# A Macaron block with RWKV-7 mixer: SP loads in a planned order, the first 128 rows first in the head, and the last 128 rows' output shared by three engines

## The chip, the cores and the metric

The kernel runs on one core of one Trainium2 chip. The time is that of one execution on the device, in microseconds; a lower time is better. The median of 3 runs of the kernel before is 2033.16 us (2027.96, 2033.72 and 2033.16).

The page of the profile names five engines: PE (TensorE, the matrix engine; its weight loads are listed apart as PEld), DVE (VectorE), ACT (ScalarE), POOL (GpSimd) and SP (SyncE, which only issues transfers). Sixteen DMA engines move the data for all of them.

## The reference

There are 256 tokens of width 2048, all in float32. Three sublayers are added to the residual stream `h` in turn:

```python
f = _swiglu(_rmsnorm(h, ffn1_pre), gate1, up1, down1);  h = h + 0.5 * _rmsnorm(f, ffn1_post)
m = _hybrid_mixer(_rmsnorm(h, mix_pre), ...);           h = h + _rmsnorm(m, mix_post)
f = _swiglu(_rmsnorm(h, ffn2_pre), gate2, up2, down2);  h = h + 0.5 * _rmsnorm(f, ffn2_post)

def _swiglu(x, wg, wu, wd): return (silu(x @ wg) * (x @ wu)) @ wd        # D_FF = 5632

def _hybrid_mixer(u, ...):
    z_a, z_b, g_a, g_b = split(u @ w_in)           # 3360, 1024, 2048 and 2048 columns
    y_a = _rwkv7_branch(z_a, ...) @ w_proj_a       # 16 heads of 64, a recurrence over the tokens
    y_b = _pool_branch(z_b, ...) @ w_proj_b        # means over windows of 2, 4, 8 and 16 tokens
    return (sigmoid(g_a) * y_a + sigmoid(g_b) * y_b) @ w_out
```

## The kernel before

**Products in three parts.** Every float32 operand is split into two parts of a shorter float format, high and low. A weight tile `w` comes from DRAM; ScalarE casts it to `wH`; VectorE subtracts to get `wL`. The activations have `xH` and `xL` in the same way. A product is then three matmuls (`mm3`: high by high, low by high, high by low). The input of each product is 128 rows of the contraction by 128, and the other operand is 512 wide. The 256 tokens are two halves `h` of 128 rows. The tile names in the rows tell the stage: `f` and `l` are the gate and the up product and, in the down product, two column groups; `mm` is a product with the token rows on the output's partitions; `tr` is a transpose on TensorE; `pS`, `pA`, `pk`, `Z`, `mz` belong to the mixer's recurrence, the "chain".

**The planner.** Nothing is issued as the program text stands. Each engine call (`Engine.__getattr__`, line 78, which is why nearly every row of the profile carries line L477, where the plan is written out) is recorded by `Plan.add` with a cost (`Plan.cost`), a nominal time `nom` (the sum of the paces of the main stream of matmuls so far) and a slack `lag`. `Plan.deadlines` gives it a due time `dl` from those who use its result. `Plan.simulate` then walks through time with a model of the five engines and the buffers, and on each engine but TensorE takes the operation with the earliest due time that is ready in the model; `Plan.emit` writes the five orders out. On TensorE the main stream keeps the program's order, and two other streams ("side" for transposes, "chain" for the recurrence) are slipped in. In the real execution each engine works strictly through its written order, so an instruction that waits holds all behind it. In the model a transfer takes its bytes at 387 per ns and lands `LAND` = 1600 ns later. `s.set(lag=..., behind=...)` changes slack, or adds a dependence, for what is recorded inside it.

**Buffers.** `w` has 5 buffers, `wH` and `wL` 5 each; all larger temporaries share 34 "units".

**Stages.** `Kernel.ffn` runs the gate and up products in 11 blocks of 512 columns, then `down`. The first gate block of the first FFN is preceded by `head` (line 675): it loads `x` in four column pieces `c` for each of the two row halves (`load(h, c)`), transposes them (`turn(h, c)`), fetches (`get`) and splits (`split(k)`) the weight tiles, and calls `do(k, h)`, the three matmuls of contraction tile `k` for row half `h`. Sixteen transposes of an identity (`WARM`) run first, and eight more (`WARM2`) behind `turn(1, 0)`. The activation of a block returns to the transposed layout by a round trip to DRAM: the tile `T` is stored to `cx` and loaded back as `x` (`carry`), then cast to `xH`/`hH` on ScalarE.

`Kernel.mixer` runs the parts of `MIX_ORDER` and, in `ev_pa`, multiplies the gate tile `sga` by `y_a @ w_proj_a` and adds `mb`, the gated second branch, which had been stored to DRAM (`msp`). The first two of the four column blocks return by `carry`, the last two by transposes (`tr<-ident,sga`). Then comes `w_out`.

**Loads from GpSimd.** `post` (line 1082) ends each sublayer: it loads the norm's weights `gb` as a broadcast row, calls `reload()` (the residual rows `xr`, `h1`, `h2`, four transfers of 512 KB by `load_to`), and after the last column group finishes the four 128x512 output pieces of each half: `fg * r + resid` on VectorE, followed by `emit`, which in the last sublayer stores to `out`. The loads of `gb`, `mb` and the reloads are issued from GpSimd's queue. All weights, `cx` and the stores to `out` go from SP; in the head the pieces `c = 0` of `x` go from ScalarE. `setup_mixer` (the mixer's constant columns, `cols`, and their transposes `pr`) is run from `s.after` behind the first up product.

Of the kernel before, what the change touches and what calls it, by code (L numbers as in the profile page):

```python
# [82 lines left out]
SYNC = 55.0  # L83
LAND = 1600.0
SWITCH = 170.0
RUN = 16
# [7 lines left out]
class Plan:  # L94
# [109 lines left out]
    def cost(s, o, name, w, r, k):  # L204
# [33 lines left out]
        elif o.eng == "DVE":  # L238
            f = 1 / 0.96
            if name in ("tensor_copy", "tensor_scalar") and not psum:  # L240
                f /= 2
            more = 45.0 if name == "scalar_tensor_tensor" else 26.0 if name == "transpose" \
                else 40.0 if name == "tensor_tensor_scan" or n < 256 else 0.0
            o.pace, o.dur = n * f + 75 + more, n * f + 158 + more
        else:
            o.pace = o.dur = {"tensor_tensor": 400 + 160.0 * n,
                              "tensor_copy": 450.0}.get(name, n + 110.0)
# [35 lines left out]
    def simulate(s):  # L283
# [20 lines left out]
        gate = {e: [] for e in engines}  # L304
        prog, cfg, held = 0.0, (0, 0), None

# [35 lines left out]
        def go(o):  # L342
# [20 lines left out]
            if o.nbytes:  # L363
                dma = max(now + 1900, dma) + o.dur
                o.end = dma + LAND
            else:
                o.end = now + dur
# [21 lines left out]
        while done < len(ops):  # L389
            moved = True  # L390
            while moved:
                moved = False
                for e in engines:
                    if free[e] > now:
                        continue
                    w, av = wait[e], avail[e]
# [94 lines left out]
class Block:  # L491
    def __init__(s, tc, ctx):
# [3 lines left out]
        s.n = 0  # L496
        s.after = []
        s.cp = E(tc.tile_pool(name="cp", bufs=1))
# [176 lines left out]
    def head(s, w, c0, KT, do, keep, xs):  # L675
# [10 lines left out]
        for _ in range(WARM):  # L686
            s.nc.tensor.transpose(ps[:, :P], s.ident, s.ident)
        load(None, None)
        load(0, 0)
        load(1, 0)  # L690
        for k in range(4):
            get(k, 1)
        for c in range(1, 4):
            load(0, c)
            get(4 * c, 2)
            load(1, c)
            get(4 * c + 2, 2)
        split(0)
        turn(0, 0)
        split(1)  # L700
        last = turn(1, 0)
        split(2)
        split(3)
        with s.set(behind=last):
            for _ in range(WARM2):
                s.nc.tensor.transpose(ps[:, :P], s.ident, s.ident)
        for k in range(KT):
            do(k, 0)
            last = do(k, 1)
            if k % 2 == 0 and k + 4 < KT:  # L710
                turn(k // 2 % 2, k // 4 + 1)
                split(k + 4)
            if k == SQ:
                late = last
        with s.set(behind=late):
# [209 lines left out]
class Kernel(Block):  # L925
# [28 lines left out]
    def ffn(s, wg, wu, wd, uT, rs, gpost, resid, emit, reload, xs=None):  # L954
# [33 lines left out]
        s.gemm_tok(wu, 0, at, NKD, hold(1))  # L988
        while s.after:
            s.after.pop(0)()  # L990
        rb = s.rtmp("rsb")
# [8 lines left out]
        for b in range(1, nb):  # L1000
            J = jobs[b]
            s.block_seq(J, jobs.get(b + 1), evac([1.0, 1.0] if b > 1 else rs, [], J.banks))
        s.down(wd, s.T_at(hT), NKF, s.post(gpost, 0.5, resid, emit, reload), hT, sm,
# [11 lines left out]
    def normed(s, uT, rb, su):  # L1015
# [66 lines left out]
    def post(s, gpost, fac, resid, emit, reload):  # L1082
# [18 lines left out]
        def ev(c, h, ps):  # L1101
            if h == 0 and c % 2 == 0:
                nc.gpsimd.dma_start(out=gb[c // 2], in_=gpost[c * 512:c * 512 + 1024]
                                    .partition_broadcast(P))
# [4 lines left out]
            if c == 3:  # L1109
                r = s.small(1, "rs", bufs=8)  # L1110
                with s.set(lag=100.0):
# [3 lines left out]
                    for q in range(4):  # L1115
                        o = cc_(fg[h], q)
                        nc.vector.scalar_tensor_tensor(out=o, in0=o, scalar=r,
                                                       in1=resid(h, q), op0=ALU.mult,
                                                       op1=ALU.add)
                        emit(h, q, o)  # L1120
                return
# [181 lines left out]
    def mixer(s, prm, uT, rs, resid, emit, gpost, reload):  # L1303
# [517 lines left out]
def kernel(tc, x, ln_ffn1_pre, ln_ffn1_post, ffn1_gate, ffn1_up, ffn1_down,  # L1821
# [11 lines left out]
    with ExitStack() as ctx:  # L1833
# [11 lines left out]
        def load(h, c):  # L1845
            if h is None:
                with s.set(lag=-20000.0):
                    nc.sync.dma_start(out=gr, in_=ln_ffn1_pre[0].rearrange("(k p) -> k p", p=P))
# [37 lines left out]

        def emit(h, c, ap):
            nc.sync.dma_start(out=out[0, h * P:h * P + P, c * 512:c * 512 + 512], in_=ap)
        s.ffn(ffn2_gate[0], ffn2_up[0], ffn2_down[0], uT3, rs3, ln_ffn2_post[0],
# [35 lines left out]
```

## Time and profile before

| | value |
|---|---|
| median of 3 runs | 2033.16 us |
| the profiled execution's own time | 2032.8 us |
| its span in the trace | 2031.1 us |
| mean granted TensorE clock | 0.995 |
| matmuls and transposes on PE | 9837 |
| moved by DMA | 470.91 MB |

The rows of the profile are quoted in the prediction. A row of the waits reads: the engine and the tile it worked on next, what ended its wait, the total in us, how often, the longest. A row of a timeline reads: start and duration in us, engine, line, operation, out<-in, count, and in brackets the idle time of the engine just before, with what ended it. A stretch (a row of the windows) gives the busy time of each engine with the number of its instructions, then the clock granted to TensorE, the busy share of the DMA engines and what they moved.

### The profile page before, as it was taken

Reading aid. Unit: us, or ns where it says so; the run is one execution under the profiler, and the core shown is the slowest. Engines: PE = TensorE matmul, PEld = TensorE weight load, DVE = VectorE, ACT = ScalarE, POOL = GpSimd, SP = SyncE. Lnnn points to the kernel's source line nnn. Section 1 sums busy time; section 2 is a strip of 40 time slices with the busy share of each in tenths; the row PEclk is TensorE's granted clock in tenths of the full one; section 3 lists DMA queues with packets and bytes.
Section 4 is the critical chain, followed back from the end, with each engine's and each line's share of the span. In section 5 each row is a group of like instructions: output and inputs, shape, how many; then the busy total and the mean of one; then the engine's idle time right before and its main releaser. Section 6 shows DMA issues by size and latency. Waiting matters only on the chain.

```text
span 2031.1 us, 28147 instructions
## 1 busy us (share of the span) xinstructions
PE 2002.6 (99%) x9837; PEld 1655.5 (82%) x9837; DVE 1744.9 (86%) x2278; ACT 1185.6 (58%) x1588; POOL 80.9 (4%) x148
## 2 busy tenths in 40 slices
PE   9999999999999999999999998999999999999998
PEld 7888888888888888887887786888888888788886
DVE  7989999999888758897868768898899999998885
ACT  7555656565555556864845444575556565655552
POOL 0000000000001110001200110010000000000000
PEclk9999999999999999999999998999999999999999
DMA  7688888887667686656575576657888888876674
GB/s 270 228 260 266 283 267 273 273 278 227 206 205 255 220 245 212 196 178 189 153 229 179 168 232 198 229 199 237 260 263 284 264 275 270 270 228 214 198 258 138
DMA packets 254855, 470.91 MB, mean 232 GB/s; under 512 B 20592, under 2 KB 43258, under 8 KB 254714
## 3 DMA queue, kind: packets, MB, share of 16 engines
q1 hardware_dynamic: 248537, 448.68, 68.5%
q0 software_dynamic: 5888, 19.93, 2.9%
q8 instruction: 77, 1.26, 0.3%
q10 hardware_dynamic: 288, 0.52, 0.1%
q14 instruction: 65, 0.52, 0.1%
HBM read 444.40 MB, written 24.64 MB: 231 GB/s over the span
## 4 chain that ended last, share of the span: by engine, by line
PE 68%; DVE 13%; DMA 8%; issue 5%; ACT 4%; SPq 1%; DVEq 0%; POOL 0%; ACTq 0%; POOLq 0%
PE l L477 23%; PE f L477 20%; PE mm L477 18%; DVE wL L477 6%; PE p L477 5%; DMA x<-cx 3%; DMA w<-in_ffn_gate_dram 3%; ACT wH L477 2%; DVE t L477 2%; SPq L477 1%; DMA w<-in_ffn_up_dram 1%; DVE w L477 1%; DMA w<-in_w_proj_a_dram 1%; DVE T L477 1%; PE tr L477 0%
## 5 line engine op out<-in xcount | busy, mean ns | idle before, releaser
L477 ACT CAST wH<-w 128x1024 fp32r<-128x1024 f32 (+2 forms) x722 | 748.2, 1047 | 625.9 <-PE mm L477 142.8
L477 DVE TENSOR_TENSOR wL<-w,wH 128x1024 fp32r<-128x1024 f32 (+2 forms) x722 | 864.6, 1211 | 162.3 <-ACT wH L477 158.5
L477 PE MATMUL l<-wL,xH 128*128 128x512 f32 x788 | 307.1, 390 | 0.0
L477 PE MATMUL l<-wH,xH 128*128 128x512 f32 x788 | 306.9, 389 | 0.0
L477 PE MATMUL l<-wH,xL 128*128 128x512 f32 x788 | 306.6, 389 | 0.0
L477 PE MATMUL f<-wL,xH 128*128 128x512 f32 x672 | 261.7, 389 | 0.2 <-DVE wL L477 0.2
L477 PE MATMUL f<-wH,xL 128*128 128x512 f32 x672 | 261.6, 389 | 0.0
L477 PE MATMUL f<-wH,xH 128*128 128x512 f32 x672 | 261.4, 389 | 0.0
L477 PE MATMUL mm<-wH,xH 128*128 128x512 f32 (+1 forms) x672 | 261.0, 388 | 0.0
L477 PE MATMUL mm<-wH,xL 128*128 128x512 f32 (+1 forms) x672 | 260.9, 388 | 0.0
L477 PE MATMUL mm<-wL,xH 128*128 128x512 f32 (+1 forms) x672 | 260.6, 388 | 0.1
L477 PEld LDWEIGHTS l<-wL,xH 128*128 128x128 f32 x788 | 147.9, 188 | 31.5 <-DVE wL L477 0.7
L477 PEld LDWEIGHTS l<-wH,xH 128*128 128x128 f32 x788 | 147.9, 188 | 30.6
L477 PEld LDWEIGHTS l<-wH,xL 128*128 128x128 f32 x788 | 147.9, 188 | 30.2
L477 DVE TENSOR_TENSOR t<-w,w 128x1024 f32<-128x1024 f32 (+1 forms) x156 | 158.5, 1016 | 16.1 <-DMA w<-in_ffn_down_dram 8.3
L477 PEld LDWEIGHTS f<-wL,xH 128*128 128x128 f32 x672 | 126.1, 188 | 27.0 <-DVE wL L477 0.7
L477 PEld LDWEIGHTS f<-wH,xH 128*128 128x128 f32 x672 | 126.2, 188 | 26.1
L477 PEld LDWEIGHTS f<-wH,xL 128*128 128x128 f32 x672 | 126.2, 188 | 26.1
L477 PEld LDWEIGHTS mm<-wH,xL 128*128 128x128 f32 x672 | 126.2, 188 | 25.0
L477 PEld LDWEIGHTS mm<-wL,xH 128*128 128x128 f32 x672 | 126.2, 188 | 25.0 <-DVE wL L477 0.5
L477 PEld LDWEIGHTS mm<-wH,xH 128*128 128x128 f32 x672 | 126.2, 188 | 24.5
L477 DVE TENSOR_TENSOR wL<-t,wH 128x1024 fp32r<-128x1024 f32 x96 | 116.8, 1217 | 5.5 <-ACT wH L477 5.1
(308 smaller groups left out, 2679.4 us busy)
## 6 DMA issues: line engine op xcount, KB each, us to landing
w<-in_w_in_dram SPq DMA_DIRECT2D x128, 512.0 KB
w<-in_ffn_up_dram SPq DMA_DIRECT2D x116, 512.0 KB
w<-in_ffn_gate_dram SPq DMA_DIRECT2D x114, 512.0 KB
w<-in_ffn_down_dram SPq DMA_DIRECT2D x112, 512.0 KB
w<-in_ffn_gate_dram SPq DMA_DIRECT2D x184, 256.0 KB
w<-in_ffn_up_dram SPq DMA_DIRECT2D x180, 256.0 KB
w<-in_ffn_down_dram SPq DMA_DIRECT2D x128, 256.0 KB
cx<-T SPq DMA_DIRECT2D x31, 512.0 KB
```

What stands on the lines that cost most here:

```text
L477: ins = o.fn(*[real(x) for x in o.a], **{n: real(x) for n, x in o.k.items()})
```

## The change

1. **The planner's model.** SP may not issue while the transfer eight back has not landed in the model (`LANES`). A transfer that depends on a transfer lands `CARRY` = 1800 ns later. GpSimd's `tensor_tensor` with 64 or more columns costs 300 + n ns instead of 400 + 160n.
2. **The queue of loads.** `gb`, `mb` and the reloads go from SP instead of GpSimd, at the place that the planner gives them. Stores to `hsp` and `msp` stay on GpSimd.
3. **The head.** All its loads carry an explicit order. The first piece of `x` comes in two halves, one from ScalarE and one from SP, and all others from SP. The products of the first 128 rows with contraction tiles 0 and 1, and the eight `WARM2` transposes, come before or around the transposes of the second 128 rows. `setup_mixer` runs at block 3, and the first additions in `normed` wait for a matmul of the head.
4. **The tail.** For the last 128 rows of the last sublayer, the first output piece is done and stored in two halves of 256 columns, and the third is multiplied on ScalarE and added on GpSimd. Each has a lag that sets its order.

The planner lays out everything anew, so that other orders change as well, the interleaving of the chain with the mixer's products among them; the main stream of TensorE changes its order only in the head.

```diff
+LANES = 8
+CARRY = 1800.0
...
-            o.pace = o.dur = {"tensor_tensor": 400 + 160.0 * n,
+            o.pace = o.dur = {"tensor_tensor": 400 + 160.0 * n if n < 64 else 300.0 + n,
...
                 o.end = dma + LAND
+                if any(ops[q].nbytes for q in o.preds):
+                    o.end += CARRY
+                if e != "POOL":
+                    lanes.append(o.end)
+                    heapq.heappush(events, (o.end, next(rel), None))
...
+                    if e == "SP" and len(lanes) >= LANES and lanes[-LANES] > now:
+                        continue
...
+        seq = itertools.count()
+
+        def first(fn, *a):
+            with s.set(lag=-30000.0 + 300 * next(seq)):
+                fn(*a)
+        first(load, None, None)
+        first(load, 0, 0)
+        first(get, 0, 1)
+        first(get, 1, 1)
+        first(load, 1, 0)
+        first(get, 2, 1)
+        first(get, 3, 1)
...
         split(0)
-        turn(0, 0)
-        split(1)
-        last = turn(1, 0)
-        split(2)
-        split(3)
+        last = turn(0, 0)
         with s.set(behind=last):
             for _ in range(WARM2):
                 s.nc.tensor.transpose(ps[:, :P], s.ident, s.ident)
+        do(0, 0)
+        split(1)
+        do(1, 0)
+        turn(1, 0)
+        do(0, 1)
+        split(2)
+        do(1, 1)
+        split(3)
...
-        while s.after:
-            s.after.pop(0)()
...
+            while s.after and b == 3:
+                s.after.pop(0)()
...
-            V.tensor_tensor(out=fl(x), in0=fl(uH).bitcast(F32), in1=fl(uL).bitcast(F32),
-                            op=ALU.add)
+            with s.set(behind=s.late):
+                V.tensor_tensor(out=fl(x), in0=fl(uH).bitcast(F32), in1=fl(uL).bitcast(F32),
+                                op=ALU.add)
...
-                nc.gpsimd.dma_start(out=gb[c // 2], in_=gpost[c * 512:c * 512 + 1024]
+                nc.sync.dma_start(out=gb[c // 2], in_=gpost[c * 512:c * 512 + 1024]
...
+                        m = 1 if q else 2
+                        for i in range(m):
+                            b = slice(i * 512 // m, (i + 1) * 512 // m)
+                            with s.set(lag=600.0 * (q + q + i) - 6000.0):
+                                if q == 2:
+                                    nc.scalar.mul(o, o, r)
+                                    nc.gpsimd.tensor_tensor(out=o, in0=o, in1=x, op=ALU.add)
+                                else:
+                                    nc.vector.scalar_tensor_tensor(
+                                        out=o[:, b], in0=o[:, b], scalar=r, in1=x[:, b],
+                                        op0=ALU.mult, op1=ALU.add)
+                                emit(h, q, o[:, b], b)
...
-                    nc.gpsimd.dma_start(out=mbs[c], in_=msp[c])
+                    nc.sync.dma_start(out=mbs[c], in_=msp[c])
...
-            (nc.sync if c else nc.scalar).dma_start(
-                out=at_tok(xs)(h, c), in_=x[0, h * P:h * P + P, c * 512:c * 512 + 512])
+            o = at_tok(xs)(h, c)
+            for q, e in ((0, nc.scalar), (1, nc.sync)) if h + c == 0 else ((None, nc.sync),):
+                b = slice(0, 512) if q is None else slice(q * 256, q * 256 + 256)
+                e.dma_start(out=o[:, b], in_=x[0, h * P:h * P + P, c * 512:c * 512 + 512][:, b])
...
-                        nc.gpsimd.dma_start(out=dst[h][c],
-                                            in_=src(h)[:, c * 1024:c * 1024 + 1024])
+                        nc.sync.dma_start(out=dst[h][c],
+                                          in_=src(h)[:, c * 1024:c * 1024 + 1024])
```

More of the change, by code (lines that the diff above doesn't have):

```diff
@@ L304, in simulate @@
         gate = {e: [] for e in engines}
-        prog, cfg, held = 0.0, (0, 0), None
+        prog, cfg, held, lanes = 0.0, (0, 0), None, []
         def can(o):
@@ L496, in __init__ @@
         s.n = 0
-        s.after = []
+        s.after, s.final = [], False
         s.cp = E(tc.tile_pool(name="cp", bufs=1))
@@ L687, in head @@
             s.nc.tensor.transpose(ps[:, :P], s.ident, s.ident)
[L688 to L692, printed above, removed]
+        seq = itertools.count()
[9 more added lines that the diff above has]
+        first(get, 3, 1)
         for c in range(1, 4):
[L694 to L697, printed above, removed]
+            first(load, 0, c)
+            first(get, 4 * c, 2)
+            first(load, 1, c)
+            first(get, 4 * c + 2, 2)
         split(0)
-        turn(0, 0)
-        split(1)
-        last = turn(1, 0)
-        split(2)
-        split(3)
+        last = turn(0, 0)
         with s.set(behind=last):
@@ L706, in head @@
                 s.nc.tensor.transpose(ps[:, :P], s.ident, s.ident)
+        do(0, 0)
[6 more added lines that the diff above has]
+        split(3)
         for k in range(KT):
-            do(k, 0)
-            last = do(k, 1)
+            if k > 1:
+                do(k, 0)
+                last = do(k, 1)
             if k % 2 == 0 and k + 4 < KT:
@@ L713, in head @@
             if k == SQ:
-                late = last
+                s.late = late = last
         with s.set(behind=late):
@@ L1115, in ev @@
                     for q in range(4):
[L1116 to L1120, printed above, removed]
+                        o, x = cc_(fg[h], q), resid(h, q)
+                        if not (s.final and h):
+                            nc.vector.scalar_tensor_tensor(out=o, in0=o, scalar=r, in1=x,
+                                                           op0=ALU.mult, op1=ALU.add)
+                            emit(h, q, o)
+                            continue
+                        m = 1 if q else 2
[8 more added lines that the diff above has]
+                                        out=o[:, b], in0=o[:, b], scalar=r, in1=x[:, b],
+                                        op0=ALU.mult, op1=ALU.add)
+                                emit(h, q, o[:, b], b)
                 return
@@ L1846, in load @@
             if h is None:
-                with s.set(lag=-20000.0):
-                    nc.sync.dma_start(out=gr, in_=ln_ffn1_pre[0].rearrange("(k p) -> k p", p=P))
+                nc.sync.dma_start(out=gr, in_=ln_ffn1_pre[0].rearrange("(k p) -> k p", p=P))
                 ps = s.psum("pg1")
@@ L1885, with emit @@
                 load_to(h1, lambda h: hsp[0, h]))
-        def emit(h, c, ap):
-            nc.sync.dma_start(out=out[0, h * P:h * P + P, c * 512:c * 512 + 512], in_=ap)
+        def emit(h, c, ap, b=slice(0, 512)):
+            nc.sync.dma_start(out=out[0, h * P:h * P + P, c * 512:c * 512 + 512][:, b], in_=ap)
+        s.final = True
         s.ffn(ffn2_gate[0], ffn2_up[0], ffn2_down[0], uT3, rs3, ln_ffn2_post[0],
```

## The prediction

> **What bounds the kernel now.** I read the page first, then the waits of TensorE, the stretches around the longest of them, and the timelines there. All times are microseconds.
>
> ```profile
> span 2031.1 us, 28147 instructions
> PE 2002.6 (99%) x9837; PEld 1655.5 (82%) x9837; DVE 1744.9 (86%) x2278; ACT 1185.6 (58%) x1588; POOL 80.9 (4%) x148
> ...
> PE tr L477 <- DVE sga L477: 8.5, 1, 8.5
> PE pS L477 <- ACT Z L477: 2.9, 1, 2.9
> PE tr L477 <- DMA x<-in_x_dram: 1.7, 1, 1.7
> PE l L477 <- DVE hL L477: 1.4, 2, 1.2
> PE pr L477 <- DMA cols<-in_pool_scale_dram: 0.5, 1, 0.5
> ```
>
> TensorE is busy for 2002.6 of 2031.1, so the kernel is bound by its matmuls. The change keeps their number and shapes. It can therefore win only in the idle 28.5 (2031.1 − 2002.6), in time at a reduced clock, and in the tail. The profiled execution took 2032.8, 1.7 more than its span and 0.4 under the median of the runs, 2033.16. I work from 2032.8. The largest idle item is one 8.5 in the mixer. What follows it is in the stretches (busy time and count of PE, PEld, DVE, ACT, POOL, then granted clock, DMA share, GB/s):
>
> ```profile
> core 0: us, PE busy (x) PEld busy (x) DVE busy (x) ACT busy (x) POOL busy (x), PEclk, DMA share, GB/s
> 945.00:950.00 5.00, 2.82 (x26) 1.75 (x24) 0.75 (x2) 1.14 (x3) 0.33 (x1) 1.00 0.95 279
> 950.00:955.00 5.00, 4.30 (x65) 3.66 (x65) 2.28 (x6) 1.33 (x3) 0.79 (x2) 0.66 0.04 11
> 605.00:615.00 10.00, 10.00 (x46) 8.29 (x45) 7.60 (x9) 5.44 (x7) 1.50 (x3) 1.00 0.95 317
> 10.00:20.00 10.00, 10.00 (x53) 8.29 (x52) 9.83 (x19) 8.90 (x24) 0.00 (x0) 1.00 1.05 399
> 1225.00:1230.00 5.00, 0.00 (x0) 0.00 (x0) 4.97 (x6) 2.51 (x3) 0.00 (x0) 0.68 0.45 152
> 1230.00:1235.00 5.00, 2.58 (x10) 2.35 (x11) 4.71 (x7) 0.76 (x2) 0.00 (x0) 0.50 0.98 277
> 1235.00:1240.00 5.00, 5.00 (x19) 4.07 (x18) 3.46 (x5) 3.33 (x5) 0.00 (x0) 0.79 0.53 166
> ```
>
> A steady stretch does 46 matmuls in 10.00, 0.217 each. After the pause the granted clock is 0.50, and 0.79 in the next 5 us, where it is still 0.5 for (1 − 0.79)/0.5 × 5 = 2.1. The pause thus costs more than itself. Why TensorE paused is in the timeline (start, duration, engine, and in brackets the idle time before it):
>
> ```profile
> 1202.64 0.53 POOL L477 DMA_DIRECT2D h<-hsp  x1 [12.42 <-DVE sga L477]
> 1203.85 0.53 POOL L477 DMA_DIRECT2D h<-hsp  x1 [0.69 <-DVE T L477]
> 1203.53 0.34 SPq L477 DMA_DIRECT2D cx<-T  x1
> 1204.58 3.77 SPq L477 DMA_DIRECT2D w<-in_w_proj_a_dram  x3
> 1208.99 2.17 SPq L477 DMA_DIRECT2D x<-cx  x4
> 1209.56 0.53 POOL L477 DMA_DIRECT2D h<-hsp  x1 [5.18 <-ACT wH L477]
> 1213.47 0.53 POOL L477 DMA_DIRECT2D gb<-in_ln_mix_post_dram  x1 [3.38 <-DVE sga L477]
> 1214.52 1.05 ACT L477 CAST wH<-w 128x1024 fp32r<-128x1024 f32 x1 [2.39 <-DMA w<-in_w_proj_a_dram]
> 1223.53 1.14 ACT L477 CAST xH<-x 128x512 fp32r<-128x512 f32 x2 [7.96 <-DMA x<-cx]
> 1232.42 1.09 PE L477 MATMUL tr<-ident,sga 128*128 128x128 f32 x4 [8.47 <-DVE sga L477]
> 1237.11 0.39 PE L477 MATMUL mm<-wL,yH 128*128 128x512 f32 x1
> ```
>
> ScalarE works in order. Its cast of x stands ahead of weight casts, and waits 7.96 for x<-cx, which SP had issued from 1208.99: 12.4 from the end of the issues (1211.16) to the cast. In that time the reloads of h and the row gb, 512 KB each and issued by GpSimd, move through the same 16 DMA engines. Behind the cast come weights, then VectorE, then the sum into sga, then TensorE.
>
> **The change part by part.**
>
> *Reloads and rows from SP (the mixer pause).* The written order of the changed kernel shows where they go: on SP the sequence cx<-T, three weights, x<-cx stays, with none of the four h loads near; these stand some twenty SP transfers further on, among weights of w_out, and one gb load stands behind this x<-cx. GpSimd no longer issues them, so x<-cx competes with SP's own three weights only. It then lands 3 to 5 after its issues end, an estimate from the 399 GB/s above: 1.3 for its own 512 KB, and at most 3.9 for the three weights ahead. ScalarE finds it at 1214 to 1216; the cast before it ended at 1214.52 + 1.05 = 1215.57. The 7.96 goes, hence the 8.47 on TensorE, and the half clock from 1232.42 to about 1237.1, which costs 4.7 × 0.5 = 2.3. I take −10.8 (0 if x<-cx is late by itself). Next late would be the w_out weights behind gb; their margin is below, with rival C.
>
> *The first pause of the chain (pS, 2.9).*
>
> ```profile
> 948.86 1.30 ACT L477 ACTIVATE mz<-x,cols 128x256 f32<-128x256 f32 x3 [3.97 <-DMA x<-cx]
> ```
>
> The same kind of pause, at 948: ScalarE waits 3.97 for a carried x, and the Z that TensorE needs is behind it. The planner now adds 1800 ns to transfers that depend on transfers, and in the changed order Z and a weight cast stand ahead of this mz. The 2.9 goes, and of the clock of 0.66 in the 5 us after it (lost: 0.34 × 4.30 = 1.5) most. I take −3.4 of 4.4; 0 is the other end, if Z then waits for something else.
>
> *The carries in the FFNs (hL, 1.4).* They are cast one weight later by the same constant. −1.0 (0 to −1.4). *pr (0.5)*: its column loads and transposes move back to a block three later; −0.3 (+0.5 to −0.5), the load then coming long before its use.
>
> *The chain written anew.* The planner lays the scan's small matmuls and copies differently. The trace of before has no row for these waits; the ends are its nearest rows: a new pause of the size of pS (+2.9), or those of its small rows gone (−3). I take +1.5, nearer to the bad end, since 65 short matmuls in 5 us each have a consumer and a producer on another engine.
>
> *The head.*
>
> ```profile
> 0.80 0.90 ACTq L477 DMA_DIRECT2D x<-in_x_dram  x2
> 6.03 0.37 ACT L477 ACTIVATE xH<-tr,g 128x128 fp32r<-128x128 f32 x1 [3.01 <-DVE g L477]
> 6.29 0.61 ACT L477 CAST wH<-w 128x512 fp32r<-128x512 f32 x1
> 7.46 0.66 PE L477 MATMUL tr<-ident,x 128*128 128x128 f32 x4 [1.68 <-DMA x<-in_x_dram]
> 7.95 1.04 PE L477 MATMUL warm<-ident 128*128 128x128 f32 x8
> 8.74 0.48 PE L477 MATMUL mm<-wH,xH 128*128 128x512 f32 x1
> ```
>
> TensorE waits 1.68 for the second 128 rows before its first product at 8.74. In the changed order the eight warm transposes and the products of the first rows come before that transpose. Their needs, xH and wH, are ready at 6.29 + 0.61 = 6.90 or a little later (SP issues a half of x first, 0.45), so the first product could start at 7.0 to 7.4. The weights that follow need 1.5 MB (1 MB of weights, 0.5 MB of x) per 24 products × 0.217 = 5.2, 288 GB/s, under the 399 shown. I take −1.5 (0 to −1.7).
>
> *The tail.*
>
> ```profile
> 936.75 1.22 POOL L477 COPY Z<-ev 64x256 f32<-64x256 f32 x1 [0.18 <-DVE T L477]
> 938.01 0.39 POOL L477 COPY Z<-od 64x256 f32<-64x256 f32 x1
> L477 ACT ACTIVATE sga<-mm,rs x8: 676/688/692, 1103.7 to 1190.6; 128x512 f32<-128x512 f32 x8
> 2023.91 0.55 POOL L477 TENSOR_TENSOR rs<-rt,mhalf 128x1 f32<-128x1 f32 x1 [10.31 <-DVE rt L477]
> 2024.49 2.74 DVE L477 SCALAR_TENSOR_TENSOR fg<-fg,rs,h 128x512 f32<-128x512 f32 x4
> 2025.27 2.32 SPq L477 DMA_DIRECT2D out_dram<-fg  x4
> ```
>
> Before: four VectorE pieces of 0.685 end at 2027.23, SP's last issue at 2027.59, the span 3.5 later. After: VectorE has the first piece in two halves (an estimate from 2.74/4 by size with the fixed part left: 0.8 together) and two whole ones, ending near 2026.7. ScalarE multiplies the third piece, 0.69, from 2024.5 to 2025.2. GpSimd then adds it; no row has that add. From the copies, 0.39 and 1.22 for 256 columns, 512 columns take 0.8 to 2.4, so it ends at 2026.0 to 2027.6. SP has the store of that third piece ahead of those of the second and fourth, so both are queued behind the GpSimd add: three issues of 0.45 later SP is done at 2027.4 to 2029.0, against 2027.59. That is −0.2 to +1.4; I take +0.5, between the two, since neither row is an addition of two operands. [...]
>
> **The sum.** −10.8 − 3.4 − 1.0 − 0.3 + 1.5 − 1.5 + 0.5 = −15.0; 2032.8 − 15.0 = 2017.8.
>
> **The rivals.**
>
> *A, the forecast:* 2017.8, between 2011 (chain −3 instead of +1.5, tail −0.2, head −1.7, hL −1.4) and 2024 (first chain pause kept, tail +1.4, no gain in the head).
>
> *B, the carry is late by itself.* The change then does not do what it says: x<-cx waits for its cx and three weights, not for h. For it: ScalarE already waited 2.39 for the weight ahead at 1214.52, and at 948.86 a carry was 3.97 late. Against it: four loads of 512 KB are 2.1 MB, 5.3 at 399 GB/s, most of the 7.96. Then the 10.8 stays, and 2032.8 − 15.0 + 10.8 = 2028.6: no change.
>
> *C, slower: the reloads hold back weights.* On SP they stand in one line with the weights. Before, GpSimd's transfers shared the engines with them. A burst of four loads and gb is 2.5 MB, 6.3 at 399 GB/s, in three places: both FFN downs and w_out. It decides where the burst exceeds the lead of the weight behind it. In the changed order that weight is used 88 matmuls after its buffer comes free and cast some 34 before: 54 × 0.217 = 11.7 against 5.3 to 6.3, which speaks against it. If the lead were nil, each place would cost 6.3 and about 1.7 of slow clock (in the ratio 2.3 to 8.47): +24, 2032.8 − 15.0 + 24 = 2041.8. [...]
>
> *D, the new order of the chain pauses by itself.* Two new pauses like that of pS, 4.4 each with the clock: 2017.8 + 8.8 = 2026.6.
>
> **How the numbers follow.** A 0.70, B 0.09, C 0.11, D 0.10. Range: 2010 to 2029, which takes in A, B and D with A's lower end and one more on that side, and leaves out C and strays. A measurement tells 0.3% from no change, 6.1 here: faster is under 2027.1, slower over 2039.3. Faster: A and three quarters of D, 0.77; same: B, the rest of D and C's milder half (one burst alone, +8, is 2025.8; two are 2033.8), 0.12; slower 0.11.
>
> **What would show it.** Right: no wait of TensorE for sga over 1, ScalarE's xH<-x near 1216 without a wait above 1, clock 1.0 through that stretch, first product near 7.2, TensorE idle about 16. Wrong: f, l or mm waiting for wL behind a DMA of w right after the h and gb loads (C), the 8 still there (B), waits in the chain by other names (D), or the last stores issued after 2027.6 relative to the same last matmul (tail).

## The result, and the profile after

| | before | after |
|---|---|---|
| median of the first 4 runs each | 2031.35 us (2027.96 to 2033.72) | 2019.05 us (2017.06 to 2021.55) |
| ratio of the runs, 95% interval | | 0.9941 [0.9921, 0.9961] |
| profiled execution, its span | 2032.8 us, 2031.1 us | 2021.55 us, 2019.8 us |

The kernel is faster by 12.3 us in the medians, where 2017.8 us had been forecast. Measured later, side by side with e9 and e11, the changed kernel took 2019.95 us (6 runs) against 2033.54 us (11 runs), a ratio of 0.9929 [0.9916, 0.9943]. The profiled execution of the changed kernel is the slowest of its first four.

The page of the profile after, and its waits of TensorE:

```profile
span 2019.8 us, 28108 instructions
PE 2001.6 (99%) x9837; PEld 1653.4 (82%) x9837; DVE 1743.5 (86%) x2278; ACT 1185.9 (59%) x1589; POOL 68.8 (3%) x127
```

```profile
PE pk L486 <- DVE nb L486: 2.0, 1, 2.0
PE l L486 <- DVE fg L486: 1.7, 2, 0.9
...
PE tr L486 <- DMA x<-in_x_dram: 1.0, 1, 1.0
...
PE tr L486 <- DVE sga L486: 0.2, 1, 0.2
PE l L486 <- DVE hL L486: 0.2, 1, 0.2
```

TensorE is busy for the same time with the same number of instructions; its idle time fell from 28.5 to 18.2 us. The waits for sga (8.5 to 0.2), Z (2.9, gone from the list) and hL (1.4 to 0.2) went. Two took part of their place: pk waits 2.0 us, and two l products wait for fg.

To see where the time went, the span is cut at fixed products. TensorE's main stream has 8448 products named f, l, mm and p, in all these kernels in the same order by their names; each number is the time between the starts of two of them, read from the trace and counted from 0. The cuts are: product 3500 (the chain begins), 4475 (between its halves), 4990 and 5025 (around the transposes of sga), 5275 (w_out is done), and the last one. The tail is what is left of the span, which is rounded to 0.1.

| profile | to 3500 | chain 1 | chain 2 | sga | w_out | FFN2 | tail | span |
|---|---|---|---|---|---|---|---|---|
| before | 803.10 | 271.41 | 145.43 | 19.67 | 57.61 | 725.19 | 8.69 | 2031.1 |
| after | 801.30 | 272.73 | 142.25 | 8.88 | 60.31 | 724.77 | 9.56 | 2019.8 |
| e1, loads from SP alone | 803.00 | 272.53 | 146.07 | 10.39 | 58.12 | 723.59 | 9.41 | 2023.1 |
| e2, hold in the plan alone | 802.95 | 273.87 | 145.89 | 20.82 | 57.61 | 722.96 | 8.69 | 2032.8 |
| e3, planner alone | 802.83 | 272.31 | 142.81 | 16.30 | 57.61 | 722.96 | 8.68 | 2023.5 |
| e4, head alone | 803.30 | 269.85 | 145.21 | 19.84 | 57.59 | 723.28 | 8.63 | 2027.7 |
| e5, reloads held on GpSimd | 803.95 | 269.85 | 144.81 | 9.35 | 57.99 | 725.15 | 8.70 | 2019.8 |
| e6, after with reloads spread | 801.92 | 271.09 | 142.25 | 8.88 | 57.61 | 725.07 | 9.56 | 2016.4 |
| e7, after with the old tail | 801.71 | 272.67 | 142.41 | 8.88 | 57.61 | 722.95 | 9.47 | 2015.7 |
| e8, after with the old head | 800.78 | 271.09 | 142.39 | 8.88 | 57.61 | 724.75 | 9.70 | 2015.2 |
| e9, after with nb early | 801.61 | 266.36 | 144.31 | 9.51 | 57.61 | 723.09 | 9.40 | 2011.9 |
| e10, after without the addition | 801.70 | 271.21 | 142.39 | 8.88 | 57.61 | 723.61 | 9.31 | 2014.7 |
| e11, e9 with the old head and tail, reloads spread | 803.84 | 266.35 | 144.38 | 8.91 | 59.22 | 724.05 | 9.25 | 2016.0 |
| e12, after once more | 801.50 | 272.83 | 142.37 | 8.85 | 59.35 | 723.03 | 9.58 | 2017.5 |

From before to after the stretches give −1.8, +1.3, −3.2, −10.8, +2.7, −0.4 and +0.9: together −11.3, the difference of the spans. The row of e2, in which every engine works through the tiles in the order of before, shows how far one execution moves by itself: +2.5 us in the chain's first half, where the clock fell to half once more than in before, and −2.2 in the second FFN.

The two columns of the chain have to be added up. The same 32 small matmuls `pA<-AR,BK` stand behind product 4475 before (which starts at 1074.51) and ahead of it after (1074.03):

```profile
1075.74 0.49 PE L477 MATMUL pA<-AR,BK 64*128 64x128 f32 x2
1076.45 2.05 PE L477 MATMUL pA<-AR,BK 64*128 64x128 f32 x30 [0.23 <-DVE AR L477]
```

```profile
1068.51 2.06 PE L486 MATMUL pA<-AR,BK 64*128 64x128 f32 x32
```

TensorE has 1663 instructions in the first half and 1067 in the second before, 1695 and 1035 after. Its chain instructions in the second half take 24.21 us before and 21.26 after, so some 3 us only change sides. Both halves together take 416.84 before and 414.98 after: −1.9.

The stretch at sga after, in the timeline:

```profile
1199.82 0.34 SPq L486 DMA_DIRECT2D cx<-T  x1
1200.88 3.81 SPq L486 DMA_DIRECT2D w<-in_w_proj_a_dram  x3
1204.79 1.84 SPq L486 DMA_DIRECT2D x<-cx  x4
1212.34 1.14 ACT L486 CAST xH<-x 128x512 fp32r<-128x512 f32 x2 [1.15 <-DMA x<-cx]
1213.37 0.41 SPq L486 DMA_DIRECT2D gb<-in_ln_mix_post_dram  x1
1258.15 0.90 SPq L486 DMA_DIRECT2D h<-hsp  x2
```

The same sequence of SP as before, without GpSimd's transfers in it. The x<-cx is there 5.7 us after its last issue ended (1206.63 to 1212.34) instead of 12.4, ScalarE waits 1.15 instead of 7.96, and the h loads leave from 1258 us on, where the quoted ones of before left at 1203 to 1210.

### The profile page after: what moved, and what is told of

Same layout as the page of the kernel before. It is cut to its first block, busy times and chain, and to the rows that moved or that the text cites. A ratio compares the mean times of both kernels' runs of the same rounds, so it can differ in the third digit from the quotient of the medians.

```text
span 2019.8 us, 28108 instructions
## 1 busy us (share of the span) xinstructions
PE 2001.6 (99%) x9837; PEld 1653.4 (82%) x9837; DVE 1743.5 (86%) x2278; ACT 1185.9 (59%) x1589; POOL 68.8 (3%) x127
## 3 DMA queue, kind: packets, MB, share of 16 engines
q8 instruction: 77, 1.26, 0.3%
## 4 chain that ended last, share of the span: by engine, by line
PE 84%; DVE 6%; DMA 4%; ACT 3%; issue 3%; SPq 0%; POOL 0%; DVEq 0%; ACTq 0%; POOLq 0%
PE l L486 29%; PE f L486 26%; PE mm L486 22%; PE p L486 5%; DVE wL L486 3%; DMA w<-in_ffn_gate_dram 2%; ACT wH L486 1%; DMA w<-in_w_out_dram 1%; DVE t L486 1%; PE tr L486 1%; SPq L486 0%; PE pY L486 0%; DMA h<-hsp 0%; DVE w L486 0%; DVE xL L486 0%
```

## The experiments

Each experiment is compared with runs of the kernel before that were made beside it, on the same chip; the chips of e1 to e4, e5 to e8 and e9 to e12 differ.

**e1: the loads from SP alone.**

```diff
 # the kernel before, with these changes only
-                nc.gpsimd.dma_start(out=gb[c // 2], ...
+                nc.sync.dma_start(out=gb[c // 2], ...
-                    nc.gpsimd.dma_start(out=mbs[c], in_=msp[c])
+                    nc.sync.dma_start(out=mbs[c], in_=msp[c])
-                        nc.gpsimd.dma_start(out=dst[h][c], ...
+                        nc.sync.dma_start(out=dst[h][c], ...
```

> The kernel before with part 2 alone: gb, mb and the reloads go from SP, the planner's model, the head and the tail stay. Theory 1 (the mixer pause came from the h reloads and gb running ahead of x<-cx from GpSimd's queue): TensorE's 8.5 us wait for sga goes to under 1 us and the 2.3 us of half clock behind it with it, the carry behind it loses up to 3 us again in w_out, where the weights now stand behind the reloads; about 9 us under before, 2022. Theory 2 (x<-cx is late by itself, the planner's new constants took the pause away): the 8.5 us stay, 2031 or above. The pS pause of 2.9 us near 948 us stays under both.

2024.84 us (9 runs) against 2033.11 (19 runs), ratio 0.996 [0.9943, 0.9976]. Its waits:

```profile
PE pS L477 <- ACT Z L477: 2.7, 1, 2.7
...
PE tr L477 <- DVE sga L477: 1.6, 2, 1.3
```

The pause at sga goes, 9.3 us in its stretch, with the planner as it was: by the trace TensorE, VectorE and ScalarE work through the tiles in the order of before, and only the issues of SP and GpSimd differ. The pause at pS stays. Theory 1's sign and size hold. w_out lost only 0.5 us of the 3 allowed, and that 0.5 stands at the second transposes of sga, at 1240 us, ahead of the reloads, which SP issues from 1265 us on.

**e2: a hold that existed in the plan only.**

```diff
+                b = back and [o for o in s.plan.ops if o.eng == "PE" and o.stream == "main"][-back]
+                with s.set(behind=b or s.plan.behind):
+                    ...  # the four reloads, from GpSimd
-                load_to(h1, lambda h: hsp[0, h]))
+                load_to(h1, lambda h: hsp[0, h], 200))
```

> The kernel before, with the four h reloads of the mixer still issued from GpSimd, but held there until a matmul of the third and fourth w_out columns is done (near 1250 us instead of 1190 to 1210 us). Nothing else moves. Theory 1: x<-cx is alone with SP's weights, the 8.5 us wait for sga goes or falls under 2 us, and GpSimd's reloads share the DMA engines later with the weights of w_out: 2020 to 2023. Theory 2 (the carry is late by itself, or GpSimd's gb alone delays it): 5 to 8 us of the wait stay, 2027 to 2031. Against the version with these loads on SP, the waits of the w_out products for fg, 1.7 us there, should be under 0.5 us if it is the place in SP's line that makes them.

2032.73 us (10 runs), ratio 0.9996 [0.9985, 1.0006]. The timeline tells why it decides nothing between the theories:

```profile
1205.40 0.53 POOL L477 DMA_DIRECT2D h<-hsp  x1 [12.42 <-DVE sga L477]
1206.62 0.53 POOL L477 DMA_DIRECT2D h<-hsp  x1 [0.69 <-DVE T L477]
...
1227.39 1.14 ACT L477 CAST xH<-x 128x512 fp32r<-128x512 f32 x2 [8.30 <-DMA x<-cx]
```

The reloads left as early as before. In this kernel `behind` only tells the planner to place an operation later; the emitted program carries no wait for it. GpSimd has almost nothing else to do (80.9 us busy of the 2031.1 before), and the four reloads left at 1192.46, 1205.40, 1206.62 and 1212.73 us, as soon as PE mm, DVE sga, DVE T and ACT wH had released them, whatever time the plan gave them. On SP the place in the order holds (1265 us in e1), because SP has weights to issue first (twelve of w_out from 1244.72 to 1264.71 us). So e2 is a repeat of the kernel before.

**e3: the planner's model alone.** The first diff hunks of the change (LANES, CARRY, the price of `tensor_tensor`) and nothing else.

> The kernel before with part 1 alone: the planner's model (LANES, CARRY, GpSimd's price), all queues, head and tail as before. Theory 1: the pause at sga stays at 6 to 9 us; the pS pause of 2.9 us near 948 us goes, as the carry is expected later there, and so does the 1.2 us wait for hL near 1744 us; 2 to 5 us under before, 2026 to 2029. Theory 2 (the planner's constants removed the pause at sga too): 2017 to 2021.

2025.01 us (5 runs), ratio 0.9956 [0.9939, 0.9973].

```profile
PE tr L486 <- DVE sga L486: 5.3, 1, 5.3
PE pk L486 <- DVE nb L486: 2.0, 1, 2.0
```

The pause at sga shrinks by 3.2 us but stays, the pause at pS goes, and pk's takes its place. More than theory 1 expected, less than theory 2: 3.4 us in the stretch at sga and 1.7 us in the two halves of the chain together (416.84 to 415.12; the 32 `pA` matmuls change sides here too). That 1.7 need not be the planner's: e4 and e5, with the planner of before, take 415.06 and 414.66, as no half clock followed pS in them. A further 2.2 us lie in the second FFN, where e2 has them as well.

**e4: the head alone** (with `setup_mixer` at block 3 and the additions of `normed` behind a matmul).

> The kernel before with part 3 alone: the head's order of loads and products, setup_mixer at block 3, the additions in normed behind a matmul of the head. Theory 1 (the head's gain was eaten where the transpose of the second 128 rows slipped in ahead of the second product): first product near 6.6 us, second near 8.4 us, and 25 products on TensorE is 0.3 to 0.7 us ahead of before; with the pr transposes out of the head 1.2 to 1.6 us ahead after the first block. Theory 2 (the 2.1 us by which the first product comes earlier are kept): 2 us ahead at 25 products and later.

A single run, 2029.37 us. The first product starts at 7.55 us, the second at 8.22, the 25th (counted from 0) at 15.19; up to product 3500 nothing is gained (803.30). Theory 1, but for the first product, which it had at 6.6, and for the 1.2 to 1.6 us after the first block: the 100th product is 1.8 us ahead, and by product 750 that is gone, with 0.7 us of waiting for a wL and 0.5 us before the moved pr transposes.

**e5: the reloads held on GpSimd by data.**

```diff
                 if h == 0:
+                    s.gate = ss[0][:, 1:2]
                     reload()
...
+                        if gate:
+                            nc.gpsimd.tensor_copy(dst[h][c][:, :1], s.gate)
                         nc.gpsimd.dma_start(out=dst[h][c], ...
```

> The kernel before, with a real hold on GpSimd: one column of each h buffer of the mixer is first copied by GpSimd from the sums of w_out's second column group, so that the four reloads, still from GpSimd, can't leave before about 1260 us. In e2 the hold existed in the plan alone and the loads left at 1192 to 1213 us as before. Theory 1 (the reloads ahead of x<-cx made the pause): the 9 us wait for sga falls to 1 to 3 us, as gb from GpSimd still shares the engines; the stretch from the last w_proj_a product to the first of w_out shrinks by 6 to 9 us, about 2025. Theory 2 (x<-cx is late by itself): the wait stays above 7 us, 2032. In w_out TensorE should lose under 1 us if only the place in SP's line makes weights late, 2 to 3 us if the bytes do.

2024.77 us (4 runs) against 2035.67 (7 runs), ratio 0.9951 [0.9934, 0.9968].

```profile
1202.18 0.34 SPq L477 DMA_DIRECT2D cx<-T  x1
1207.09 1.85 SPq L477 DMA_DIRECT2D x<-cx  x4
...
1214.02 1.14 ACT L477 CAST xH<-x 128x512 fp32r<-128x512 f32 x2 [0.51 <-DMA x<-cx]
```

Here the wait is real. Nothing was given to SP, its order is that of before and so is the planner, yet x<-cx is there 5.1 us after its issues (1208.94 to 1214.02), ScalarE waits 0.51, and the sga stretch takes 9.35 us. So GpSimd's transfers in flight beside x<-cx made the pause, not the carry itself. Reloads and gb are not told apart: with the reloads out of its way the second gb left at 1188.34, where it left at 1213.47 before. The reloads left from 1280 us on, later than intended; the 0.4 us that w_out lost stand at the second transposes of sga, at 1236 us, ahead of them.

**e6: the mixer's reloads later on SP.**

```diff
+                main = [o for o in s.plan.ops if o.eng == "PE" and o.stream == "main"]
                 for h in range(2):
+                    with s.set(behind=main[-back[h]] if back else s.plan.behind):
+                        ...  # the two loads of half h
-                load_to(h1, lambda h: hsp[0, h]))
+                load_to(h1, lambda h: hsp[0, h], (60, 1)))
```

> The changed kernel with the mixer's h reloads later on SP: the first row half among the last five weights of w_out, the second half among the first weights of the second FFN. Theory 1 (the burst of four reloads and gb in SP's line makes the weights of w_out late): the 1.7 us wait for fg and its neighbours go, w_out takes 2.7 us less, about 2016.4. Theory 2 (w_out is slower for another reason, the bytes or the changed order of casts): no change, 2019.

2018.01 us (4 runs), ratio 0.9923 [0.9903, 0.9943] to before. w_out takes 57.61, as theory 1 said. But e7 to e10, whose reloads stand where the changed kernel has them, take 57.61 too, and e12 takes 59.35. So the 2.7 us of the first profile come in some executions of the same order. Of the 2.7 and of the 1.7 us of e12, 0.4 each stand at the second transposes of sga, the rest around the l products that wait for fg (two, and one in e12), some 20 us behind the reloads. Whether e6 cures that rest is not decided: e6 and e11, with the reloads spread, do not have it, and four of the six profiles without e6's edit do not either. What it looks like, in the windows of the changed kernel, and last, for comparison, the middle one of e7:

```profile
1265.00:1270.00 5.00, 5.00 (x24) 4.14 (x23) 3.49 (x5) 2.62 (x3) 0.00 (x0) 1.00 1.03 386
1270.00:1275.00 5.00, 5.00 (x24) 4.14 (x23) 1.81 (x2) 2.11 (x2) 0.00 (x0) 1.00 0.88 335
1275.00:1280.00 5.00, 4.75 (x21) 3.59 (x20) 4.17 (x6) 1.63 (x3) 0.00 (x0) 1.00 0.29 100
...
1270.00:1275.00 5.00, 5.00 (x24) 4.14 (x23) 3.44 (x4) 2.11 (x2) 0.00 (x0) 1.00 0.76 283
```

Behind the reloads and gb the DMA engines are full (1.03, 386 GB/s), VectorE runs dry (1.81 of 5 us, 3.44 in e7), and then everything it owes comes at once.

**e7: the tail of before in the changed kernel.**

> The changed kernel with the tail of before (four pieces on VectorE). Theory 1 (the GpSimd addition holds VectorE): each VectorE piece takes 0.75 us again instead of one at 1.81 us, and from the last matmul's start to the end it is 8.7 us instead of 9.6 us: 0.9 us less, 2018.2. Theory 2 (the tail's length comes from the stores' landing alone): 9.3 us or more.

2017.35 us (4 runs), ratio 0.9919 [0.99, 0.9938]. The groups of the tail by shape, first of the changed kernel, then of e7:

```profile
L486 DVE SCALAR_TENSOR_TENSOR fg<-fg,rs,h 128x512 f32<-128x512 f32 x2 | 2.5, 1273 | 0.0
L486 POOL TENSOR_TENSOR fg<-fg,h 128x512 f32<-128x512 f32 x1 | 1.3, 1262 | 0.8 <-ACT fg L486 0.8
L486 DVE SCALAR_TENSOR_TENSOR fg<-fg,rs,h 128x256 f32<-128x256 f32 x2 | 0.9, 480 | 0.1
```

```profile
L486 DVE SCALAR_TENSOR_TENSOR fg<-fg,rs,h 128x512 f32<-128x512 f32 x4 | 2.7, 746 | 0.1
```

The pieces on VectorE take 0.75 us again, as theory 1 said, and the last store is issued at 4.85 us after the start of the last product instead of 5.38. The tail's length is theory 2's, 9.47 us: SP sees the last store landed at 7.53 us instead of 8.10, and then needs 1.9 us to the end of the span, where the changed kernel needs 1.5, and before 1.1. That closing takes 1.1 us in the five profiles whose reloads come from GpSimd and 1.1 to 2.0 us where SP issues them. What makes it was not tried. The time does not tell e7 from the changed kernel (0.9919 beside 0.9929 to before).

**e8: the head of before in the changed kernel.**

> The changed kernel with the head of before (load order, products two by two, warm transposes behind the second transpose), but setup_mixer still at block 3. Theory 1 (the head's new order is worth nothing, the gain of the first 100 products was the pr transposes that left it): the 25th product starts at 14.7 to 15.1 us, against 15.4 us, and the time is the same within 1 us or up to 0.5 us better. Theory 2 (the head gained 1.5 us): 25th product near 15.9 us, 1 to 2 us slower, 2020.5.

2019.33 us (4 runs), ratio 0.9926 [0.9908, 0.9944]: the same time within the spread. The 25th product starts at 14.83 us and product 3500 at 800.78, the earliest of all. Theory 1; but e11, with the same head, is the latest of all at the 25th (17.13) and has gained nothing by product 3500 (803.84).

**e9: nb early.**

```diff
-        V.tensor_copy(nb, n2.unsqueeze(2).to_broadcast([P, 16, 64]))
+        with s.set(lag=-12000.0):
+            V.tensor_copy(nb, n2.unsqueeze(2).to_broadcast([P, 16, 64]))
```

> The changed kernel with one line moved: VectorE's broadcast copy nb of the second chain, which TensorE's pk transposes wait for 2.0 us at 1017 us, gets its due time 12 us earlier and stands some 25 VectorE instructions earlier. Theory 1 (pk waits only because nb stands behind a wL that waits for its cast): the 2.0 us wait goes, and with it the chance of 3.4 us at half clock behind it, 2 to 3.7 us less, about 2016.5. Theory 2 (the chain is late by its own length there): the wait comes back at the next step of the chain, 2019.

2014.20 us (4 runs, 2013.25 to 2014.98), ratio 0.9903 [0.9889, 0.9916], against 2019.95 for the changed kernel on the same chip. The copy and the transposes, in the changed kernel and in e9:

```profile
1016.78 0.69 DVE L486 COPY nb<-n 128x1024 f32<-128x1024 f32 x1
...
1017.61 1.06 PE L486 MATMUL pk<-ident,nb 128*128 128x128 f32 x8 [2.02 <-DVE nb L486]
```

```profile
988.13 0.69 DVE L486 COPY nb<-n 128x1024 f32<-128x1024 f32 x1
989.34 1.03 PE L486 MATMUL pk<-ident,nb 128*128 128x128 f32 x8
```

The transposes come 28 us earlier and wait for nothing. The chain's two halves take 4.3 us less (272.73 + 142.25 − 266.36 − 144.31): theory 1. Some 1.6 of that is half clock behind the pause, which the changed kernel's profile has and those of e6, e8 and e10 do not have; against these e9 takes 2.7 to 2.9 less. It is not the price of this wait alone either, as the planner laid the chain out anew and several hundred instructions of TensorE stand elsewhere. This one line makes the fastest kernel of the study by its median, 5.8 us under the changed one. Of the 5.6 us between the profiles of e12 and e9 the chain has 4.5 and w_out 1.7.

**e10: the tail without the GpSimd addition.**

> The changed kernel without the GpSimd addition in the third output piece of the last 128 rows (ScalarE's product is stored alone, so h is left out of that piece). Theory 1 (the GpSimd addition and VectorE's instruction with two SBUF operands exclude each other): VectorE's pieces take 0.48, 0.48, 0.75 and 0.75 us, none 1.81 us, and the last store is issued near 4.4 us after the start of the last matmul, against 5.4 us. Theory 2 (ScalarE's write of the same buffer, or the stores' reads, slow VectorE): one piece stays above 1.2 us.

A single run, 2016.47 us; by its edit the third piece lacks the residual. VectorE's pieces:

```profile
L486 DVE SCALAR_TENSOR_TENSOR fg<-fg,rs,h 128x512 f32<-128x512 f32 x2 | 1.4, 744 | 0.0
```

None is held, and the last store is issued at 4.49 us. Theory 1, as far as the addition goes: with ScalarE's work on the same buffer alone the pieces take 0.74 us, GpSimd's addition costs VectorE 1.06 us (1.81 − 0.75). Whether the two SBUF operands make the difference is not shown, as no run varies them.

**e11: everything together** (old head, old tail, reloads spread, nb early).

> The changed kernel with the head of before, the tail of before, the h reloads of the mixer spread as in e6 and nb early as in e9. By the runs so far: head 0.6 us, nb 2 to 3.7 us, the tail nothing or a little, the reloads 0 to 2.7 us: 2014 to 2016, if the terms add up; a rival is that the laid-out order of the chain moves again and gives 1 to 3 us back, 2017 to 2018.

2014.44 us (5 runs, 2013.30 to 2017.68), ratio 0.9908 [0.9895, 0.9921]. Not better than e9 alone: the other three edits add nothing that these runs can tell. The profiled execution is the slowest of the five. Its chain is that of e9 (410.73, 410.67 there); its head comes late, and its w_out loses 1.6 us where TensorE waits 1.4 us for sga, at 1232 us, not behind the reloads.

**e12: the changed kernel once more.**

> The changed kernel once more, on the same chip as e9 and e11, for comparison: 2017 to 2021. If the 2.7 us lost in w_out in its first profile belong to that execution only, the stretch of the w_out products is 57.6 us here; if they belong to the kernel, 60.3 us.

2019.95 us (6 runs). w_out takes 59.35 us, between the two values, with one wait left:

```profile
PE l L486 <- DVE fg L486: 0.8, 1, 0.8
```

## Why the prediction was right, and where its steps were wrong

**The mixer pause: right in cause and size.** GpSimd's transfers in flight made x<-cx late. −10.8 had been forecast, and the stretch at sga lost 10.79 us. e5 shows the cause: holding the reloads back, with nothing else of the change, takes 10.3 us off; e1, with the queue alone, 9.3. Rival B (the carry late by itself) falls with them. What the prediction had not seen is that the planner's new constants alone take a third of it (e3, 3.4 us); the parts do not add up. The landing of x<-cx, estimated at 3 to 5 us after its issues, took 5.7 (5.1 to 6.9 in e1, e5, e9, e11 and e12), and ScalarE still waited 1.15 us. Of the other signs, TensorE's wait for sga (0.2) and the clock (1.0) came as said, the first product came at 6.61 for 7.2, and TensorE was idle for 18.2 for 16.

**The chain: right in sum, with two terms that were both too large.** −3.4 for the first pause and +1.5 for the new order had been forecast, −1.9 together, and both halves together lost 1.9. The wait at pS (2.9) went as forecast. The slow clock did not: 3.41 us at half clock followed pS before and follow pk after. The new order did pause anew, as rival D had it, but by less than a pause of 4.4: pk waits 2.0 us instead of 1.2, because nb stands behind a wL on VectorE, and pB waits 0.5. So most of the −3.4 was won, the clock's share of it was not, and the +1.5 was too dear; that the sum fits to 0.1 is luck. Where the clock stayed whole, both halves take 414.66 and 415.06 with the planner of before (e5, e4), 413.3 to 413.6 in e6, e8 and e10, but 415.12 in e3, which has the planner's part alone and another wait of 1.0 us at pSa.

**The head: the step failed; the row it was read from comes in some executions only.** The 1.68 us wait of the transpose, and the first product at 8.74, are not there in e1, e2 and e3, which have the same head: first product at 7.31 to 7.63, 25th at 14.71 to 15.04. With the new head the 25th product starts at 14.90 to 15.80 in seven profiles, with the old one at 14.71 to 17.13 in seven, median 15.19 and 15.04. So the new head is not earlier. The two latest with the old head are before (15.91) and e11 (17.13). In e11 TensorE waits 1.01 us for x, and it is also slow until about 10 us: its eight warm transposes take 1.91 us, where they took 1.04 before.

```profile
7.21 1.11 PE L486 MATMUL tr<-ident,x 128*128 128x128 f32 x4 [1.01 <-DMA x<-in_x_dram]
8.12 1.91 PE L486 MATMUL warm<-ident 128*128 128x128 f32 x8
```

Whether the new order guards against such a late head, these runs do not show. The new order gains little because of the transpose of the second 128 rows, which the planner slips in ahead of the second product:

```profile
6.61 0.47 PE L486 MATMUL mm<-wH,xH 128*128 128x512 f32 x1
...
8.04 0.66 PE L486 MATMUL tr<-ident,x 128*128 128x128 f32 x4 [0.96 <-DMA x<-in_x_dram]
...
8.45 0.48 PE L486 MATMUL mm<-wL,xH 128*128 128x512 f32 x1
```

The first product comes 2.1 us earlier, and TensorE then waits in front of the second one for x after all. What was gained before product 3500 (−1.8, which is also what head and pr had been given) came with the whole change: head alone (+0.2) and planner alone (−0.3) have next to none of it, the old head with the rest of the change has 2.3 in e8 and none in e11. Which part brings it is not shown.

**hL: also one execution's.** The second FFN took 2.2 us more in before than in e2, and no wait for hL above 0.2 us is left in e2, e3 and e4, of which only e3 has the constant that was to remove it. The second FFN takes 722.95 to 725.15 us in the other profiles, with and without the change. The −1.0 had been promised to the change and was owed to the next execution.

**w_out: rival C came, in small.** w_out lost 2.7 us in the first profile, 2.3 of it behind the reloads, and 1.7 and 1.3 in e12; it lost nothing in e7 to e10, which have the reloads in the same place. The forecast's margin of 11.7 against 6.3 us was right for most executions and is thin in some. That a weight behind a reload on one queue waits for the whole of it was the author's estimate; no run here isolates it: e5, with the reloads on another queue, lost nothing behind them, but they left 20 us later there.

**The tail: +0.9 for +0.5, and only part of it by the step that was priced.** The forecast went by the last store's issue, and that came 0.5 us later: 5.38 us after the start of the last product instead of 4.86. The terms differ. GpSimd's addition took 1.26 us, within the 0.8 to 2.4 allowed, but VectorE's piece beside it took 1.81 instead of 0.75, which the sum did not have: the two started together at 2.89 us after the last product's start, and the piece took 1.06 us more than alone, most of the 1.26. In e10, without the addition, it took 0.74. The other 0.4 us came behind the last store's landing, where the sum had nothing; e1 and e7, with the tail of before and the reloads on SP, take 9.41 and 9.47 us as well. Between e7 and the changed kernel, which differ in the order of the pieces alone, lies 0.1 us.

The sum came out at −15.0 against −11.3 in the two profiles and −12.3 in the medians. Of the 3.7 us missing in the profiles w_out has 2.7, the second FFN 0.6 and the tail 0.4; the terms up to sga agree in sum, the main one by its cause, the others by misses that cancel. Two of the prediction's figures do not come out of its own terms, without changing the forecast: what it names for the lower end of 2011 gives 2012.0, and the milder half of C is named under "same", but its chance is counted under "slower", while one burst alone, 2025.8, lies under the bound of 2027.1 for "faster".

## What to carry to other kernels

A planned time held here only on a queue that had something to do before it: on SP the reloads left at 1265 us (e1), on GpSimd, planned for about 1250 us, from 1192 us on (e2). And the transfers in flight held up what was urgent: x<-cx came 12.4 us after its issues with them beside it (before), and 5.1 us with them held back (e5). When a stall is removed, look for what is scheduled just behind it: here a broadcast copy that can run 28 us earlier stood behind other work of VectorE, and the kernel with that line moved was 5.8 us faster, beside 13.6 for the whole change on the same chip. Before two stretches are compared, count that the same instructions lie in them: 32 matmuls on the other side of a cut looked like a loss of 1.3 and a gain of 3.2 us. Before a wait of 1 to 2 us in a single profile is given a price, see whether a second execution has it.

## What the runs showed of the hardware

**After the same pause the clock fell in some executions and not in others.** Between the first 11 us and the last stretch before the end, the granted clock is at half for 3.41, 6.83 or 10.24 us at a time in before, after, e1 to e4, e7 and e12, and never in the others. After the same 2.0 us pause of pk it dropped for 3.41 us in after, e7 and e12 and stayed whole in e3, e6, e8 and e10; after the pause at pS it dropped at 2.9, 2.7 and 1.9 us (before, e1, e2) and not at 2.4 and 2.2 us (e5, e4). TensorE has the same order of tiles in after, e6, e7, e10 and e12. The stretches behind pk, in after and then in e6:

```profile
1015.00:1020.00 5.00, 2.98 (x16) 2.31 (x15) 5.00 (x9) 1.17 (x2) 0.00 (x0) 0.90 0.88 273
1020.00:1025.00 5.00, 5.00 (x19) 3.99 (x18) 4.89 (x7) 1.36 (x2) 0.00 (x0) 0.76 0.54 167
```

```profile
1015.00:1020.00 5.00, 3.01 (x18) 2.35 (x17) 5.00 (x9) 1.67 (x2) 0.00 (x0) 1.00 0.90 278
1020.00:1025.00 5.00, 5.00 (x23) 4.13 (x22) 4.99 (x8) 2.36 (x3) 0.00 (x0) 1.00 0.53 176
```

The first half of the chain shows the price: 272.7 to 272.8 us with the drop, 271.1 to 271.2 us without (after, e7 and e12 against e6, e8 and e10). The two longer drops lasted two and three times the 3.41 us, and those behind pS and pk followed pauses of 1.9 to 2.9 us, shorter than the shortest drop. What sets the length, and when a pause brings a drop, is not shown.

**The GpSimd addition cost VectorE more than it saved.** It took 0.75 us of VectorE's work away and added 1.06 us to another piece: the longest piece took 1.81 us in after, e9 and e12, beside an addition of 1.26 us, and 0.75 us in e7, e10 and e11, which have none.
